# DeltaNet heads two at a time in lockstep, and windowed attention pipelined over its blocks

## The chip, the cores and the metric

The kernel runs on one core of one Trainium2 chip. Its time is the device time of one execution in microseconds; the median of several executions is given. The engines of the core work beside each other, each through its own queue in order: PE is TensorE (matrix products, results in PSUM), DVE is VectorE, ACT is ScalarE, POOL is GpSimd, and SP issues most of the DMA transfers.

## What is computed

One inference step of two layers over a prompt of 2048 tokens with 16 learned tokens ahead of it, and 8 sample tokens with states of their own. Layer AB projects its input once and feeds two branches: A, attention with a window of 128 positions, 8 query heads and 2 key heads; B, a gated DeltaNet of 4 heads. Layer C is a gated linear attention of 4 heads. The part that the change reorders, cut from the reference:

```python
def _gated_delta_chunked(q, k, v, beta, g, s0, lead):
    ...
    a_mat = jnp.where(strict, jnp.einsum('bnhik,bnhjk->bnhij', kbeta, kc) * decay, 0.0) + jnp.eye(CHUNK, dtype=F32)
    ...
    sol = lax.linalg.triangular_solve(a_mat, rhs, left_side=True, lower=True, unit_diagonal=True)
    ...
    def step(S, xs):
        u_c, w_c, qk_c, qd_c, kd_c, gl_c = xs
        v_new = u_c - jnp.einsum('bhck,bhkv->bhcv', w_c, S)
        o = jnp.einsum('bhck,bhkv->bhcv', qd_c, S) + jnp.einsum('bhij,bhjv->bhiv', qk_c, v_new)
        S = S * gl_c[..., None, None] + jnp.einsum('bhck,bhcv->bhkv', kd_c, v_new)
        return S, o

    S, o = lax.scan(step, s0.astype(F32), xs)

def _sink_attend(q, k, v, mask, sink):
    s = jnp.einsum('...qhgd,...khd->...hgqk', q.astype(F32), k.astype(F32)) * (A_HEAD_DIM ** -0.5)
    ...
    p = p / (jnp.sum(p, axis=-1, keepdims=True) + jnp.exp(sk - m))
    o = jnp.einsum('...hgqk,...khd->...qhgd', p, v.astype(F32))
```

## The kernel before

The tokens go through in four groups of 512; group 0 carries 24 more columns, the sample and the learned tokens. For each group the kernel does layer AB, its output projection (`ab_out`), layer C and its output projection.

Most of TensorE's work are the projections. `proj` (L492) takes each product in three matmuls, of a high and a low part of the weights and of the input, into PSUM tiles named `pp` (four of them). This is called bulk here. The rest goes into PSUM tiles named `pc`, in short bursts: for DeltaNet (`dn_head`, L1420) and for attention (`swa_pair`, L983). These are generators that run as side streams of the bulk: `bulk` (L399) adds the planned time of each piece of a projection to a clock, and whenever the clock has passed the due time of a stream it lets this stream emit its next step, which then says how long it is planned to take (the numbers of `DEF_LAT`, L32). Streams of one kind stand in a lane, one after another: a lane `dn` for the heads of DeltaNet, a lane `swa` for the pairs of attention heads. `join` (L418) emits steps until given streams have ended, with no bulk ahead of them. `ORDER` (L30) is the order in a group: the convolution and gates of a head (`c1`, `c2`, `c3`; `c0` comes ahead) in turn with the attention pairs (`s0` to `s3`). What is emitted so is then ordered on each engine by a scheduler, within its dependences. So the order on an engine is found from the planned clock, the due times and the pools.

Tiles of 512 columns (`T`, 52 of them, 47 to be taken by streams), and the larger `BQ` tiles (4) are counted by `take` and `give`; a stream that finds none waits in `take_in`, which steps on the clock by 0.5. Smaller pools are `t512` (4), `sm` (20) and `inv` (6).

A head of DeltaNet goes through these steps for the group's four chunks of 128 at once: transposes and norms of keys, the products of keys with keys and queries (`BQ`), an inversion of the triangular matrix (L1496 on), transposes of values and queries; then the scan, chunk by chunk, and a normalisation (L1608 to L1616) with the gate. The inversion starts with blocks of 32: in four stages, s = 2, 4, 8, 16, TensorE does 16 matmuls of 32x32 for the four chunks (`pc<-inv,t`), DVE multiplies with a mask (`Pm`), TensorE does 16 more (`pc<-inv,inv`), and DVE subtracts (`Yn`) and transposes (`X`). In the profile a matmul in fp32 shows as two records, so a burst of 16 is 32. In the scan a chunk needs the state S (`pc<-S,CQ`), a DVE operation (Z), a matmul (`pc<-t,t`), a copy on ACT, two more matmuls (`pc<-t,t`, `pc<-t,BQ`), and the new S on DVE.

A pair of attention goes over four blocks of 128 queries. `scores` is four matmuls (`pc<-kh,t`), then a maximum on DVE, the exponential on ACT and a division on DVE; `values` transposes the probabilities on TensorE (L1015) and copies them on ACT (L1017); `out` is the products with the values (`pc<-t,va`).

## Time and profile before

| | |
|---|---|
| median of 3 runs | 2223.04 us (2221.27 to 2227.0) |
| the profiled execution | 2224.94 us |
| its span, first to last instruction | 2223.2 us |
| granted TensorE clock, mean | 0.986 |
| HBM traffic | 297.19 MB read, 101.70 MB written, 179 GB/s over the span |

Busy time is the time in which an engine had an instruction under way. Matmuls overlap, so TensorE can be busy and still not at its peak. A row of a group gives line, engine, operation, output and inputs by name without buffer numbers, shape, count, then busy time, mean ns of one, and the idle time of the engine ahead of them with what ended it. A row of the timeline gives start, duration, the same names, a count where several stand in a line, and in brackets the idle time ahead of it.

### The profile page before, as it was taken

How to read it: one execution, taken by the hardware profiler on the slowest of the kernel's cores; microseconds unless marked ns; L12 is line 12 of the kernel's file. 1: busy time of each engine (PE TensorE's matmuls, PEld its weight loads, DVE VectorE, ACT ScalarE, POOL GpSimd, SP SyncE). 2: the span in 40 equal slices, each digit the busy share in tenths (PEclk: the TensorE clock that was granted, in tenths of full speed). 3: DMA queues.
4: the chain of work that ended last, by engine and by line, in shares of the span. 5: the costliest groups of instructions: out<-in, count | busy, mean ns of one | idle time of the engine just before them, and what ended most of it. 6: DMA issues, size and time to landing. Idle time of an engine off the chain costs nothing.

```text
span 2223.2 us, 43787 instructions
## 1 busy us (share of the span) xinstructions
PE 2152.0 (97%) x17290; PEld 1809.8 (81%) x17290; DVE 1231.0 (55%) x3501; ACT 835.4 (38%) x2235; POOL 263.6 (12%) x314
## 2 busy tenths in 40 slices
PE   8889999999999999999999999999999999999997
PEld 8878888888879777788887777788887877778886
DVE  7768876655464566544344466545344466654323
ACT  5435444443352244333332244334333233334222
POOL 0011100021210011002220011002130000001111
PEclk9989999999999999999999999999999999999999
DMA  6643537767766723464555733365554743274444
GB/s 236 211 155 121 175 118 263 253 218 261 253 204 244 242 96 103 135 239 142 181 204 164 267 107 102 125 218 169 180 198 147 245 147 114 86 259 156 157 149 156
DMA packets 162622, 400.17 MB, mean 180 GB/s; under 512 B 22048, under 2 KB 54464, under 8 KB 162384
## 3 DMA queue, kind: packets, MB, share of 16 engines
q1 hardware_dynamic: 162416, 397.37, 52.6%
q8 instruction: 136, 2.23, 0.4%
q14 instruction: 70, 0.57, 0.1%
HBM read 297.19 MB, written 101.70 MB: 179 GB/s over the span
## 4 chain that ended last, share of the span: by engine, by line
PE 69%; DVE 5%; DMA 2%; ACT 2%; issue 2%; POOL 1%; SPq 0%; DVEq 0%; POOLq 0%; ACTq 0%
PE pp L110 53%; PE pc L110 14%; DVE t L116 2%; DVE t L113 1%; DVE inv L113 1%; PE pc L1015 1%; DMA t<-in_xT 1%; PE pc L1796 1%; DMA t<-x2d 1%; POOL sm L206 0%; DVE t L120 0%; DVE t L999 0%; PE pc L1575 0%; PE pc L1450 0%; DMA t<-rows 0%
## 5 line engine op out<-in xcount | busy, mean ns | idle before, releaser
L110 PE MATMUL pp<-t,wh 128*128 128x512 f32 (+1 forms) x4528 | 1265.8, 364 | 17.7 <-DVE t L113 7.7
L110 PEld LDWEIGHTS pp<-t,wh 128*128 128x128 f32 x4528 | 782.6, 191 | 128.4 <-issue 19.6
L110 PE MATMUL pp<-t,wl 128*128 128x512 f32 (+1 forms) x2264 | 808.8, 358 | 1.9 <-DVE wl L113 1.7
L110 PEld LDWEIGHTS pp<-t,wl 128*128 128x128 f32 x2264 | 429.8, 190 | 60.5 <-DVE wl L113 2.7
L113 POOL TENSOR_TENSOR t<-t,t 128x512 fp32r<-128x512 f32 (+3 forms) x128 | 163.8, 1298 | 517.3 <-ACT t L660 275.1
L110 PE MATMUL pp<-wh,t 128*128 128x256 f32 (+1 forms) x1088 | 209.0, 288 | 3.8 <-DVE QKt L113 3.8
L116 DVE SCALAR_TENSOR_TENSOR t<-t,PV,t 128x512 f32<-128x512 f32 (+4 forms) x232 | 176.0, 768 | 60.0 <-ACT t L1098 24.3
L110 PEld LDWEIGHTS pp<-wh,t 128*128 128x128 f32 x1088 | 172.4, 190 | 6.0 <-DVE QKt L113 4.0
L206 POOL TENSOR_TENSOR sm<-sm,mh 128x2 f32<-128x2 f32 (+3 forms) x84 | 68.4, 814 | 812.3 <-DVE sm L116 367.5
L116 DVE SCALAR_TENSOR_TENSOR t<-pp,t 128x512 f32<-128x512 f32 (+3 forms) x160 | 93.1, 586 | 120.0 <-PE pp L110 67.5
L110 PE MATMUL pp<-wl,t 128*128 128x256 f32 (+1 forms) x544 | 155.8, 286 | 0.0
L113 DVE TENSOR_TENSOR wl<-raw,wh 128x512 fp32r<-128x512 f32 (+3 forms) x138 | 92.2, 685 | 23.3 <-PE pp L110 10.9
L110 PEld LDWEIGHTS pp<-wl,t 128*128 128x128 f32 x544 | 103.4, 190 | 0.6
L365 ACT CAST wh<-raw 128x512 fp32r<-128x512 f32 (+2 forms) x122 | 68.0, 588 | 50.6 <-DMA raw<-in_w_c 17.0
L113 DVE TENSOR_TENSOR t<-t,t 128x512 f32<-128x512 f32 (+4 forms) x103 | 62.9, 614 | 41.3 <-ACT t L489 40.0
L113 DVE TENSOR_TENSOR QKt<-pp,t 128x512 f32<-128x512 f32 (+1 forms) x40 | 23.3, 586 | 111.0 <-PE pp L110 95.6
L110 PEld LDWEIGHTS pc<-t,t 128*128 128x128 f32 (+4 forms) x496 | 62.9, 162 | 22.2 <-DVE t L116 4.0
L489 ACT ACTIVATE t<-t 128x512 f32<-128x512 f32 (+1 forms) x70 | 44.1, 631 | 97.5 <-DVE t L116 69.0
L1004 ACT ACTIVATE t<-t,sm 128x257 f32<-128x257 f32 x128 | 64.2, 504 | 43.4 <-DVE sm L116 42.7
L110 PE MATMUL pc<-t,t 128*128 128x128 f32 (+5 forms) x496 | 78.1, 267 | 1.6 <-DVE t L116 0.8
L113 DVE TENSOR_TENSOR t<-pp,t 128x268 f32<-128x268 f32 (+1 forms) x90 | 44.4, 497 | 50.3 <-PE pp L110 36.0
L1017 ACT COPY t<-pc 128x512 f32<-128x512 f32 x64 | 37.5, 586 | 79.5 <-PE pc L1015 77.7
(334 smaller groups left out, 2806.5 us busy)
## 6 DMA issues: line engine op xcount, KB each, us to landing
wh<-wd SPq DMA_DIRECT2D x157, 512.0 KB, 3.6
wl<-wd SPq DMA_DIRECT2D x157, 512.0 KB, 4.5
wd<-wh SPq DMA_DIRECT2D x55, 512.0 KB, 4.0
wd<-wl SPq DMA_DIRECT2D x55, 512.0 KB, 5.6
t<-in_xT SPq DMA_DIRECT2D x72, 256.0 KB, 4.6
raw<-in_w_ab SPq DMA_DIRECT2D x25, 512.0 KB, 5.7
raw<-in_w_c SPq DMA_DIRECT2D x16, 512.0 KB, 4.9
out_yp<-t SPq DMA_DIRECT2D x32, 256.0 KB, 2.5
```

Of the source, the lines that this page charges most:

```text
L110: T.matmul(out, lhsT, rhs, start=start, stop=stop)
L113: return (eng or V).tensor_tensor(out, a, b, op=op)
L116: V.scalar_tensor_tensor(out, a, s, b, op0=op0, op1=op1)
L206: G.tensor_tensor(out, x, mh[0:x.shape[0]].to_broadcast(list(x.shape)), op=ALU.pow)
L365: last[0] = A.copy(hi[:, c], raw[:, c])
L489: A.activation(sq[:, :q.C], x, AF.Square)
L1004: A.activation(S_[:, kv], S_[:, kv], AF.Exp, bias=st[:, 2 + kv:3 + kv], accum_out=st[:, 4 + kv:5 + kv])
L1015: T.transpose(pt[:, kv, x], S_[:, kv, 128 * x:128 * x + 128], ident)
L1017: A.copy(PT, pt)
L1796: T.transpose(oT[:, c], On[:, c, 128 * j:128 * j + 128], ident)
```

## The change

A new function `together` takes the streams of several heads and advances all of them by one step at a time; its step is planned to take the longest of theirs times `PAIR_LAT`, 1.25. In `ab_conv` the main chunks of heads 0 and 1, and of 2 and 3, are collected and spawned as one stream when the second of them has its queries and keys. The streams of the 16 learned tokens (group 0 only) stay one per head. A wait inside such a stream now yields `None`, which steps on by 0.5 and lets the other head of a pair wait with it.

`swa_pair` emits, for every pair but the last of `ORDER` (u = 3), in one step the `out` of block b - 2, the `values` of block b - 1 and the `scores` of block b, six steps in all, where it took one of them per step. The last pair is as before.

`BQ` tiles go from 4 to 6, `t512` from 4 to 8, `sm` from 20 to 24, `inv` from 6 to 10, and a scratch buffer for DMA descriptors is set to 1024. No arithmetic changes.

```diff
+NBQ = 6
+PAIR_LAT = 1.25
...
+    def together(gens):
+
+        gens = list(gens)
+        while gens:
+            lat, pe = [], 0.0
+            for gen in list(gens):
+                r = next(gen, False)
+                while r and r[0] is None:
+                    yield r
+                    r = next(gen, False)
+                if r:
+                    lat.append(r[0])
+                    pe += r[1]
+                else:
+                    gens.remove(gen)
+            if lat:
+                yield max(lat) * PAIR_LAT if len(lat) > 1 else lat[0], pe
...
         while not cond():
-            yield 0.5, 0.0
+            yield None, 0.0
...
-                s = spawn(chunks(), "dn", LAT["dn_spawn"], tag=h)
-                q.dn.append(s)
+                q.pair.append(chunks())
+                if h % 2:
+                    q.dn.append(spawn(together(q.pair), "dn", LAT["dn_spawn"], tag=h))
+                    q.pair = []
...
+        if u == int(ORDER[-1][1]):
...
+        else:
+
+
+            PT = {}
+            for i in range(6):
+                if i >= 2:
+                    out(i - 2, PT.pop(i - 2))
+                if 1 <= i <= 4:
+                    PT[i - 1] = values(i - 1)
+                if i < 4:
+                    scores(i)
+                if i == 3:
+                    give("T", 2)
+                yield LAT["sw_p"], (1.35 if 2 <= i <= 3 else 0.9 if i in (1, 4) else 0.45)
...
-        tc4 = lambda: wk.tile([128, 4, 32], F32, tag="inv", bufs=6, name=nm("inv"))
+        tc4 = lambda: wk.tile([128, 4, 32], F32, tag="inv", bufs=10, name=nm("inv"))
...
-    nc = _bacc.Bacc("TRN2", target_bir_lowering=False, num_devices=1)
+    nc = _bacc.Bacc("TRN2", target_bir_lowering=False, num_devices=1, dynamic_dma_scratch_size=1024)
```

What this makes of the order on TensorE is shown at three places. The numbers behind a name tell instances of it apart; rows into `pp` are bulk, one matmul each. Lines of the changed kernel lie two further down here (L110 is L112).

First TensorE in the inversion of a head, group 1, before: `pc<-inv,inv` and `pc<-inv,t` are the two kinds of burst of a stage.

```order
L110 MATMUL pc_9785<-inv_9802,inv_9777 32x32 x16
L110 MATMUL pp_9968<-t_8092,wl_9832 128x512
L110 MATMUL pp_9968<-t_8103,wh_9831 128x512
L110 MATMUL pp_9968<-t_8104,wh_9831 128x512
L110 MATMUL pc_9842<-inv_9804,t_9697 32x32 x16
L110 MATMUL pp_9968<-t_8103,wl_9832 128x512
L110 MATMUL pp_9968<-t_8123,wh_9831 128x512
L110 MATMUL pp_9968<-t_8124,wh_9831 128x512
L110 MATMUL pc_9842<-inv_9859,inv_9827 32x32 x16
```

And the changed kernel in the inversion of a pair of heads, the same group (9375 and 9382 are the matrices of the two heads):

```order
L112 MATMUL pc_9524<-inv_9541,inv_9500 32x32 x16
L112 MATMUL pc_9544<-inv_9561,inv_9519 32x32 x16
L112 MATMUL pc_9613<-inv_9543,t_9375 32x32 x16
L112 MATMUL pp_9881<-t_8131,wh_9655 128x512
L112 MATMUL pc_9633<-inv_9563,t_9382 32x32 x16
L112 MATMUL pc_9613<-inv_9630,inv_9587 32x32 x16
L112 MATMUL pc_9633<-inv_9650,inv_9606 32x32 x16
L112 MATMUL pc_9707<-inv_9632,t_9375 32x32 x16
```

A burst of one head had three bulk matmuls behind it; now bursts of two heads stand in turn, with one bulk matmul in a stage here, and up to three in others.

Second, TensorE in the last scan of group 0, before, with the state S_48 of head 3 (one chunk's first bursts):

```order
L110 MATMUL pc_4421<-S_48_170,CQ_3295 128x128 x2
L110 MATMUL pp_4531<-t_103,wl_4405 128x268
L110 MATMUL pp_4531<-t_107,wh_4404 128x268
L110 MATMUL pp_4531<-t_108,wh_4404 128x268
L110 MATMUL pp_4531<-t_107,wl_4405 128x268
L110 MATMUL pp_4531<-t_111,wh_4404 128x268
L110 MATMUL pp_4531<-t_112,wh_4404 128x268
L110 MATMUL pp_4531<-t_111,wl_4405 128x268
L110 MATMUL pc_4421<-t_4270,t_3693 128x128
L110 MATMUL pp_4531<-t_115,wh_4404 128x268
L110 MATMUL pp_4531<-t_116,wh_4404 128x268
L110 MATMUL pp_4531<-t_115,wl_4405 128x268
```

And the changed kernel there, with the states S_47 and S_48 of heads 2 and 3 (a chunk, and the start of the next):

```order
L112 MATMUL pc_5091<-S_47_168,CQ_2187 128x128 x2
L112 MATMUL pc_5095<-S_48_170,CQ_3000 128x128 x2
L112 MATMUL pc_5091<-t_4987,t_4288 128x128
L112 MATMUL pc_5095<-t_4994,t_4296 128x128
L112 MATMUL pc_5109<-t_966_5100,t_3299 128x128
L112 MATMUL pc_5109<-t_966_5100,BQ_4301 128x128
L112 MATMUL pc_5114<-t_968_5105,t_4281 128x128
L112 MATMUL pc_5114<-t_968_5105,BQ_4307 128x128
L112 MATMUL pc_5119<-S_47_168,CQ_2187 128x128 x2
L112 MATMUL pc_5123<-S_48_170,CQ_3000 128x128 x2
```

The bulk matmuls between the bursts are gone here; the long run of them for the output projection follows after the normalisation of both heads. In groups 1 to 3 the scans of a pair keep bulk between them.

Third, DVE in group 0 ahead of an eviction of bulk (`t<-pp,t`), before; `sm_1804` is a small tile of the sample tokens, `wl` the low part of a weight, split on DVE from what ACT has cast to `wh`:

```order
L116 SCALAR_TENSOR_TENSOR t_367_1816<-pc_1791,sm_1804,t_366_1814 8x128
L116 SCALAR_TENSOR_TENSOR sm_1855<-sm_1855 32x1
L113 TENSOR_TENSOR t_1446<-t_1446,sm_1855 32x128
L116 SCALAR_TENSOR_TENSOR t_365_1805<-t_367_1816,sm_1804,t_365_1805 8x128
L113 TENSOR_TENSOR wl_1910<-raw_1905,wh_1909 128x512
L116 SCALAR_TENSOR_TENSOR sm_1804<-sm_1804 8x1
L113 TENSOR_TENSOR wl_2140<-raw_2135,wh_2139 128x512
L120 TENSOR_SCALAR t_365_1805<-t_365_1805,sm_1804 8x128
L113 TENSOR_TENSOR t_1831<-pp_1676,t_232 128x268
```

And the changed kernel ahead of the like eviction (`sm_1805`; `inv` and `CC` with `t_1233` and `t_1241` belong to the inversions of heads 0 and 1):

```order
L118 SCALAR_TENSOR_TENSOR sm_1805<-sm_1805,egs_196 8x1
L115 TENSOR_TENSOR inv_1785<-inv_1687,pc_1766 128x128
L118 SCALAR_TENSOR_TENSOR t_362_1817<-pc_1792,sm_1805,t_361_1815 8x128
L1563 STREAM_TRANSPOSE inv_1879<-inv_1785 128x128
L118 SCALAR_TENSOR_TENSOR sm_1829<-sm_1829 32x1
L115 TENSOR_TENSOR t_1233<-inv_1765,CC_92 128x128 x2
L118 SCALAR_TENSOR_TENSOR t_360_1806<-t_362_1817,sm_1805,t_360_1806 8x128
L115 TENSOR_TENSOR t_1204<-t_1204,sm_1829 32x128
L115 TENSOR_TENSOR t_1233<-inv_1765,CC_92 128x128 x2
L122 TENSOR_SCALAR inv_1909<-pc_1900 32x128 x2
L115 TENSOR_TENSOR t_1241<-inv_1785,CC_92 128x128 x2
L115 TENSOR_TENSOR t_1841<-pp_1567,t_232 128x268
```

The two weight splits ahead of the eviction stand further up now, ahead of the sample's operations, and steps of two inversions have come between.

## The prediction

> **What bounds the kernel now.** I read the page first, then the table of waits, then single stretches of the timeline. Lines of the page (engine busy, share of the span; then the chain that ended last):

> ```profile
> PE 2152.0 (97%) x17290; PEld 1809.8 (81%) x17290; DVE 1231.0 (55%) x3501; ACT 835.4 (38%) x2235; POOL 263.6 (12%) x314
> PE 69%; DVE 5%; DMA 2%; ACT 2%; issue 2%; POOL 1%; SPq 0%; DVEq 0%; POOLq 0%; ACTq 0%
> PE pp L110 53%; PE pc L110 14%; DVE t L116 2%; DVE t L113 1%; DVE inv L113 1%; PE pc L1015 1%; DMA t<-in_xT 1%; PE pc L1796 1%; DMA t<-x2d 1%; POOL sm L206 0%; DVE t L120 0%; DVE t L999 0%; PE pc L1575 0%; PE pc L1450 0%; DMA t<-rows 0%
> ```

> TensorE is the bound, and over half of the chain is the projections, the matmuls into `pp`, called bulk below. So the change can win only what TensorE spends beside the matmuls: places where it changes from bulk to a side burst (into `pc`) and back, and waits. Windows (length, then busy time of PE, PEld, DVE, ACT, POOL, with counts; granted clock; DMA) say where waits are:

> ```profile
> 0.00:400.00 400.00, 369.00 (x3831) 333.32 (x3832) 305.36 (x1067) 186.29 (x560) 35.33 (x51) 0.95 0.55 186
> 650.00:970.00 320.00, 314.39 (x2916) 253.70 (x2915) 186.73 (x535) 117.09 (x340) 24.72 (x38) 1.00 0.52 177
> 970.00:1170.00 200.00, 199.57 (x1144) 173.72 (x1143) 83.09 (x180) 70.90 (x151) 39.66 (x39) 1.00 0.51 177
> ```

> The first 400 us, roughly layer AB of the first group of tokens, idle 31 us; layer AB of the second (650 to 970) idles 5.6; a layer C (970 to 1170), which the change hardly touches, 0.4. The largest waits of TensorE on the parts in question (total, times, longest) and one on the timeline:

> ```profile
> PE pc L110 <- DVE inv L113: 13.4, 17, 1.8
> 143.56 0.79 PE L110 MATMUL pp<-t,wh 128*128 128x268 f32 x2 [5.92 <-DVE t L113]
> ```

> **Inversion bursts.** The order of TensorE shows 693 uninterrupted runs of bulk before and 501 after, with the same matmuls. Places where bulk is left for a 32-wide burst fall from 163 to 86: 77 fewer. The timeline of one head's inversion, second group:

> ```profile
> 668.39 0.45 PE L110 MATMUL pc<-inv,inv 32*32 32x32 f32 x32
> ...
> 668.92 0.29 DVE L113 TENSOR_TENSOR inv<-inv,pc 128x128 f32<-128x128 f32 x1 [0.50 <-PE pc L110]
> ...
> 669.25 0.28 PE L110 MATMUL pp<-t,wh 128*128 128x268 f32 x1
> 669.46 0.45 PE L110 MATMUL pc<-inv,t 32*32 32x32 f32 x32
> 669.85 0.39 PE L110 MATMUL pp<-t,wh 128*128 128x268 f32 x1
> 669.99 0.29 DVE L113 TENSOR_TENSOR inv<-pc,CC 128x128 f32<-128x128 f32 x1 [0.44 <-PE pc L110]
> 670.08 0.29 PE L110 MATMUL pp<-t,wl 128*128 128x268 f32 x1
> 670.20 0.41 PE L110 MATMUL pp<-t,wh 128*128 128x268 f32 x2
> ```

> A bulk matmul of this width starts 0.12 us after the last (670.08 to 670.20). The one ahead of the burst holds 0.21 (669.25 to 669.46), 0.09 more. The row of all such bursts gives 0.197 us for one matmul:

> ```profile
> L110 PE MATMUL pc<-inv,t 32*32 32x32 f32 x2328 | 39.8, 197 | 12.6 <-DVE inv L113 12.1 <-issue 0.2
> ```

> So the last of the 32 starts 0.45 - 0.20 = 0.25 after the first, and bulk only at 0.39: 0.14 more. The first bulk matmul then holds 0.23 (669.85 to 670.08) in place of 0.12: 0.11 more. One visit costs 0.34 us beside its work, and 77 fewer save **26 us**.

> The pair's chain works against it. From a burst's start to the DVE operation on its result is 0.53 us (668.39 to 668.92, and 669.46 to 669.99; DVE stood idle for PE both times), that takes 0.29, and DVE's end to the next PE start is 0.05 (S in the next fence: 691.87 + 0.34, then 692.26). A stage has two such halves: 2 x 0.87 = 1.74 us. After the change TensorE has, in a stage of a pair, four bursts of 0.25 and mostly one bulk matmul, with its switches about 0.46: 1.46 us. The missing 0.28 us is a new wait, over 4 stages x 2 pairs x 4 groups = 32 stages **+9 us**; 0 where two more bulk matmuls stand between, 32 x 0.74 = 24 where none does. The 13.4 us of waits listed are 17, and there are 16 heads in four groups: I read them as one at the start of each inversion. A pair has one start in place of two: half would be -7, and I take **-5** (0 to -9), since a pair's start has more to wait for.

> **Wide bursts.** The other 115 of the 192 runs saved are 128-wide bursts of the scan and attention (scan of a head, all engines):

> ```profile
> 690.81 0.49 PE L110 MATMUL pc<-t,t 128*128 128x128 f32 x2
> ...
> 691.14 0.39 PE L110 MATMUL pc<-t,BQ 128*128 128x128 f32 x2
> 691.28 0.49 PE L110 MATMUL pp<-t,wh 128*128 128x268 f32 x2
> ...
> 691.61 0.29 PE L110 MATMUL pp<-t,wl 128*128 128x268 f32 x1
> 691.73 0.41 PE L110 MATMUL pp<-t,wh 128*128 128x268 f32 x2
> 691.87 0.34 DVE L116 SCALAR_TENSOR_TENSOR S<-S,el,pc 128x128 f32<-128x128 f32 x1
> 691.98 0.29 PE L110 MATMUL pp<-t,wl 128*128 128x268 f32 x1
> ...
> 692.26 0.71 PE L110 MATMUL pc<-S,CQ 128*128 128x128 f32 x4
> ...
> 693.01 0.35 DVE L116 SCALAR_TENSOR_TENSOR t<-pc,sm,t 128x128 f32<-128x128 f32 x1 [0.60 <-PE pc L110]
> ```

> Two bulk matmuls after the burst take 0.33 (691.28 to 691.61), later 0.25: 0.08 is lost per visit. But a burst that another burst follows takes 0.33 (690.81 to 691.14), one that bulk follows 0.14: the switch is paid all the same. I take **0**, from -0.08 x 115 = -9 to +0.11 x 115 = +13.

> **The end of group 0.** Here the order shows the scan of heads 2 and 3 with no bulk at all between its bursts, where before each head's bursts had 3 to 7 bulk matmuls between. TensorE must then wait out the chain. Rows of the rest of that chain:

> ```profile
> 693.91 0.39 PE L110 MATMUL pc<-t,t 128*128 128x128 f32 x2
> ...
> 694.33 0.27 ACT L1593 COPY t<-pc 128x128 f32<-128x128 f32 x1 [1.49 <-PE pc L110]
> ...
> 695.24 0.38 PE L110 MATMUL pc<-t,t 128*128 128x128 f32 x2
> ...
> 696.13 0.35 DVE L116 SCALAR_TENSOR_TENSOR S<-S,el,pc 128x128 f32<-128x128 f32 x1
> ```

> One chunk without bulk: 0.75 to the DVE operation (692.26 to 693.01), 0.35, 0.42 from the next burst to ACT (693.91 to 694.33), 0.27, 0.89 to S (695.24 to 696.13), 0.35, and three times 0.05: 3.2 us. TensorE's own bursts are about 0.47 (690.81 to 691.28), 0.47 for S,CQ by the same spacing, and 0.2: 1.1 a head, 2.2 a pair. So 1.0 us idle in each of 4 chunks, 4 us. Then the normalisation, with all of a head's steps in a line:

> ```profile
> 699.93 0.39 PE L110 MATMUL pc<-t,BQ 128*128 128x128 f32 x2
> ...
> 701.62 1.01 POOL L206 TENSOR_TENSOR sm<-sm,mh 128x4 f32<-128x4 f32 x1 [42.06 <-DVE sm L116]
> ...
> 702.67 0.69 DVE L113 TENSOR_TENSOR t<-t,sm 128x512 f32<-128x512 f32 x1 [1.12 <-POOL sm L206]
> ```

> From the last burst to the end of the DVE product: 703.36 - 699.93 = 3.4 us, and the second head's POOL operation is 1.0 later: 4.4 us with nothing for TensorE. Before, 60 us around this place idled 3.3 us, which go:

> ```profile
> 270.00:330.00 60.00, 56.67 (x691) 49.77 (x683) 47.55 (x202) 27.37 (x95) 4.43 (x5) 1.00 0.36 114
> ```

> Net 4 + 4.4 - 3.3 = **+5** (0 to +15, if the same pair's inversion, which stands among attention bursts, waits too). In groups 1 to 3 the scan keeps 1 to 9 bulk matmuls between bursts, and only the last attention pair is left at the end with about 4 between: I take 1.3 us a group, under half of those 3.3, **+4** for the three (0 to +12).

> **The stall at 143.56 and the clock.** Its windows:

> ```profile
> 137.00:143.00 6.00, 0.64 (x5) 0.40 (x4) 4.09 (x20) 4.98 (x18) 2.16 (x3) 0.70 0.24 86
> 143.50:147.00 3.50, 3.31 (x17) 3.03 (x21) 3.37 (x11) 1.65 (x4) 0.00 (x0) 0.50 0.87 216
> 150.00:160.00 10.00, 10.00 (x264) 8.42 (x263) 6.70 (x24) 0.83 (x2) 0.00 (x0) 0.85 0.73 255
> ```

> After 5.92 us idle the clock is 0.50 from 143.5 to 147 and 0.85 over 150 to 160, which is 3 us of half speed there; with 147 to 150 between, 9.5 us at half speed, up to 4.7 us lost. The wait itself was DVE's queue: an eviction of `pp` behind operations of the sample tokens and two weight splits that wait for ACT. In the new order the splits stand further ahead of that eviction, and a pair's inversion beside it. I take half of 5.92 + 4.7: **-5** (0 to -11). The idle 4.4 us at the end of group 0 could do the same to the clock: waits up to 1.8 us left it at 1.00 and 5.9 halved it, so I take **+2** (0 to +4.7).

> [...]

> The other edits move nothing by themselves: more buffers of `BQ`, `t512`, `sm` and `inv` let two heads live at once, the smaller DMA scratch pays for them, and the polling steps issue no instruction. What they could cost is room: pairs take their tiles in a block, which is the drain below.

> **Sum.** -26 + 9 - 5 + 0 + 5 + 4 - 5 + 2 = -16 us. The profiled run took 2224.94 us (its span 2223.2); it becomes 2209. The median of the runs, 2223.04, lies 1.9 below it: **2207 us**.

> **Rivals.** (1) *The pairs' chain is the bound*: no bulk is left between the bursts of a stage, 24 in place of 9: -1 us, 2222. For it: before, DVE already waited 0.44 and 0.50 for PE in each half, so nothing is slack. Against: the order has a bulk matmul in most stages. (2) *The drain*, slower: both heads of a pair end together, so at each output projection, not only in group 0, the pair's scan and normalisation have no bulk beside them: 8.4 us idle and 4.7 of half clock in each of four groups is 52, where the sum has 5 + 4 + 2; -16 + 41 = +25, 2248. It decides where the last bulk matmul is issued before the pair's first chunk; the order shows that for group 0, and bulk in the others, which speaks against it. (3) *The waits go as well*: the stall at 143.56 and its clock wholly (-11), the inversion waits (-9), no new one in the stages (0): -16 - 6 - 4 - 9 = -35, 2188. For it: DVE is 55% busy and the two heads cover each other. That the change doesn't pair the heads is excluded by the order.

> **Numbers.** Forecast (2199 to 2216) 0.45, rival 1 (2216 to 2230) 0.22, drain 0.16, rival 3 (2180 to 2199) 0.17. A measurement tells about 0.3%, 6.7 us, from no change: faster 0.62, same 0.22, slower 0.16. The range leaves out the lower half of rival 3 and the upper part of the drain: 2190 to 2238.

> **What would show it.** Bulk entries to 32-wide bursts fall and waits of `pc` on DVE `inv` stay near 13 us: forecast; they grow by 10 or more: rival 1. Layer AB of the second group should be 5 to 7 us shorter; if it isn't, the price of a visit is wrong. Idle of TensorE before the first output projection (270 to 330) over 10 us with a clock below 1.00: the drain. The stall near 143 gone: rival 3. Wrong altogether would be a slower layer C, or waits on a DMA.

## The result, and the profile after

The changed kernel takes 2302.05 us in the median of 4 runs (2297.99 to 2310.96), beside 2222.26 us before (2221.27 to 2227.0): a ratio of 1.0363, 95% interval 1.0337 to 1.039. It is 80 us slower, where 16 us faster was forecast. The profiled execution took 2310.96 us. Its page, engine busy and the chain that ended last:

```profile
PE 2195.0 (95%) x17290; PEld 1859.5 (81%) x17290; DVE 1225.4 (53%) x3501; ACT 833.5 (36%) x2235; POOL 265.2 (11%) x314
PE 55%; DVE 5%; issue 3%; DMA 3%; ACT 2%; POOL 1%; SPq 0%; DVEq 0%; POOLq 0%; ACTq 0%
```

TensorE does the same 17290 matmuls and is busy 43 us longer; its idle time grew from 71 to 114 us. And "issue", time in which an engine waits for nothing that the profile shows, stands in the chain with 3%, where it had 2%. The table of waits of TensorE (total, times, longest) names it first:

```profile
PE pc L112 <- issue: 21.2, 17, 2.7
PE pc L112 <- DVE inv L115: 11.4, 13, 2.9
PE pp L112 <- DMA wl<-wd: 8.8, 3, 3.3
PE pc L1039 <- DVE t L122: 8.5, 14, 0.9
```

The waits on DVE's `inv`, which the prediction took as the danger, did not grow (13.4 us before). Waits on a DMA (`wl<-wd`), which it named as a sign of being wrong altogether, are new. The windows that answer to the three shown of before (the same layers, which lie later now; the columns are the window, its length, the busy time and count of PE, PEld, DVE, ACT and POOL, the granted clock, the share of DMA and its GB/s):

```profile
0.00:400.00 400.00, 361.13 (x3631) 323.17 (x3632) 290.34 (x1036) 178.46 (x544) 33.98 (x50) 0.91 0.50 168
673.00:1003.00 330.00, 314.26 (x2878) 256.38 (x2878) 180.73 (x529) 113.91 (x336) 24.91 (x37) 0.94 0.48 164
1013.00:1187.00 174.00, 173.50 (x996) 150.99 (x995) 68.82 (x149) 60.03 (x126) 38.09 (x34) 1.00 0.51 182
```

The granted clock in layer AB of the second group is 0.94 now, and was 1.00; layer C is as it was. Cut at the starts of the same bulk matmuls of the trace, near the borders of the layers, the time lies so (us; the experiments are told below). For the noise of one trace: e3 below, which has neither pairs nor the pipelined attention, differs from the kernel before by 6 us in C 0 and by under 3 in every other column.

```
                          AB 0   C 0    AB 1   C 1    AB 2   C 2    AB 3   C 3
before                    380.8  244.6  327.6  184.4  349.1  181.8  328.7  204.7
after                     405.9  242.9  346.3  184.6  369.0  181.5  350.5  205.1
e1_pair_only              402.0  238.4  340.5  185.0  369.3  180.6  340.2  205.2
e2_swa_only               380.7  237.4  328.2  185.1  346.1  184.8  325.3  204.8
e4_half_issue             400.7  240.3  327.4  185.7  351.2  180.9  328.2  204.8
e5_spread                 390.8  241.9  336.2  184.5  360.4  183.9  332.7  204.7
e6_keep_busy              392.3  239.0  341.6  184.7  362.0  181.2  343.4  204.9
e8_spread_g0_single       380.7  241.2  337.3  184.2  363.0  181.5  334.6  204.7
e9_half_g0_single         388.1  237.3  326.9  184.8  348.5  183.5  328.0  205.0
e10_before_half           383.6  242.9  327.8  184.5  346.5  180.9  327.7  205.2
e11_scan_pair             374.5  236.2  324.0  184.6  345.1  182.3  322.3  204.6
```

All four layers AB lost 19 to 25 us. The place in each is the inversion of a pair. TensorE on the timeline of the first pair of group 1 (start, length, operation, output and inputs, size, count, and in brackets the idle time ahead and what ended it):

```profile
778.09 0.45 PE L112 MATMUL pc<-inv,t 32*32 32x32 f32 x32
778.36 0.81 PE L112 MATMUL pc<-inv,inv 32*32 32x32 f32 x33
781.74 0.60 PE L112 MATMUL pc<-inv,inv 32*32 32x32 f32 x28 [2.56 <-issue]
782.13 0.24 PE L112 MATMUL pc<-inv,t 32*32 32x32 f32 x1
782.14 0.25 PE L112 MATMUL pc<-inv,inv 32*32 32x32 f32 x3
782.18 0.63 PE L112 MATMUL pc<-inv,t 32*32 32x32 f32 x31
782.74 0.80 PE L112 MATMUL pp<-t,wh 128*128 128x512 f32 x1
783.47 0.65 PE L112 MATMUL pc<-inv,t 32*32 32x32 f32 x32
783.92 0.63 PE L112 MATMUL pc<-inv,inv 32*32 32x32 f32 x32
785.46 0.65 PE L112 MATMUL pc<-inv,inv 32*32 32x32 f32 x32 [0.92 <-DVE inv L1563]
785.92 0.62 PE L112 MATMUL pc<-inv,t 32*32 32x32 f32 x32
786.47 0.80 PE L112 MATMUL pp<-t,wl 128*128 128x512 f32 x1
787.19 0.65 PE L112 MATMUL pc<-inv,t 32*32 32x32 f32 x32
```

From the one bulk matmul of a stage (782.74) to that of the next (786.47) are 3.7 us, twice the 1.74 of the prediction. TensorE breaks off at 779.2, with 33 of the 64 records of the two heads' bursts done, and goes on 2.56 us later. The second head's burst had begun, and the rest of it needs nothing that its first matmul didn't. The bulk matmul then takes 0.80 us in place of 0.50, and from 780 on the clock is at about half:

```profile
776.00:780.00 4.00, 3.05 (x153) 2.10 (x139) 2.73 (x10) 0.00 (x0) 0.00 (x0) 1.00 0.92 352
780.00:792.00 12.00, 8.69 (x324) 6.56 (x324) 5.46 (x24) 0.00 (x0) 0.00 (x0) 0.54 0.04 12
```

What breaks a burst is told by a queue that the prediction did not read. The page's part on DMA queues has an instruction queue q8; the trace has 136 records of it, 16384 bytes each, and 136 x 256 is just above 2 x 17290, the matmuls and weight loads of TensorE: blocks of 256 instructions, by division 64 bytes each. The rows above agree: from 781.74 up to 785.46 are 128 matmuls (28 + 1 + 3 + 31 + 1 + 32 + 32), with their weight loads 256 instructions, and there TensorE stops again. The profile puts these 0.92 us down to a transpose on DVE; but the next stop, at 788.92, is "issue" again and another 256 instructions on. In the whole run, stops for "issue" that follow each other in one pair's inversion stand a block apart, without exception. In the stretch above the blocks start at 779.3, 782.8, 786.6 and 790.1 us. Data transfers do not hold them up there: the window from 780 has the DMA engines busy for a share of 0.04. Over the whole run no two are closer than 3.33 us; before, the closest were 3.35. A stage of a pair is four bursts of 32 matmuls and 32 weight loads, 256 instructions: one block, 3.5 to 3.8 us. Before, a head's stage had 128 and those of 6 or 7 bulk matmuls, some 140 in 2.5 us: a block lasted by this about 4.5 us. That was enough: before, TensorE's waits for "issue" are 0.2 us, in one place.

### The profile page after: what moved, and what is told of

Its sections match the earlier page's. It is cut to its first block, busy times and chain, and to the rows that moved or that the text cites. A ratio compares the mean times of both kernels' runs of the same rounds, so it can differ in the third digit from the quotient of the medians.

```text
span 2309.1 us, 43811 instructions
## 1 busy us (share of the span) xinstructions
PE 2195.0 (95%) x17290; PEld 1859.5 (81%) x17290; DVE 1225.4 (53%) x3501; ACT 833.5 (36%) x2235; POOL 265.2 (11%) x314
## 4 chain that ended last, share of the span: by engine, by line
PE 55%; DVE 5%; issue 3%; DMA 3%; ACT 2%; POOL 1%; SPq 0%; DVEq 0%; POOLq 0%; ACTq 0%
PE pp L112 42%; PE pc L112 11%; DMA t<-x1d 2%; DVE t L118 2%; DVE t L115 1%; POOL sm L208 1%; PE pc L1039 1%; DMA wl<-wd 1%; DVE inv L115 1%; DVE t L122 1%; ACT junk L1492 1%; PE pc L1834 0%; ACT t L1028 0%; DVE t L1023 0%; DMA t<-x2d 0%
## 5 line engine op out<-in xcount | busy, mean ns | idle before, releaser
L112 PE MATMUL pp<-t,wh 128*128 128x512 f32 (+1 forms) x4528 | 1276.1, 367 | 16.2 <-ACT t L152 7.7
L112 PEld LDWEIGHTS pp<-t,wh 128*128 128x128 f32 x4528 | 803.1, 194 | 139.0 <-issue 14.1
L112 PE MATMUL pp<-t,wl 128*128 128x512 f32 (+1 forms) x2264 | 815.3, 360 | 11.6 <-DMA wl<-wd 8.8
L112 PEld LDWEIGHTS pp<-t,wl 128*128 128x128 f32 x2264 | 438.0, 194 | 73.3 <-DMA wl<-wd 10.1
L112 PE MATMUL pp<-wh,t 128*128 128x256 f32 (+1 forms) x1088 | 208.3, 287 | 3.8 <-DVE QKt L115 3.8
L112 PEld LDWEIGHTS pp<-wh,t 128*128 128x128 f32 x1088 | 171.7, 190 | 5.9 <-DVE QKt L115 4.0
L112 PE MATMUL pp<-wl,t 128*128 128x256 f32 (+1 forms) x544 | 155.4, 286 | 0.0
L208 POOL TENSOR_TENSOR sm<-sm,mh 128x4 f32<-128x4 f32 (+3 forms) x84 | 68.8, 819 | 680.8 <-DVE sm L124 279.3
L112 PEld LDWEIGHTS pp<-wl,t 128*128 128x128 f32 x544 | 103.3, 190 | 0.7
L112 PE MATMUL pc<-t,t 128*128 128x128 f32 (+5 forms) x496 | 76.5, 276 | 1.1 <-DMA t<-in_sdn 0.4
L112 PEld LDWEIGHTS pc<-t,t 128*128 128x128 f32 (+4 forms) x496 | 63.0, 170 | 14.0 <-issue 3.6
L112 PEld LDWEIGHTS pc<-inv,t 32*32 32x32 f32 x2328 | 38.5, 128 | 44.3 <-issue 29.5
```

Source lines behind the costliest of these rows:

```text
L112: T.matmul(out, lhsT, rhs, start=start, stop=stop)
L208: G.tensor_tensor(out, x, mh[0:x.shape[0]].to_broadcast(list(x.shape)), op=ALU.pow)
```

## The experiments

Three theories. *Supply*: a pair's inversion needs instructions faster than they come. *Clock*: the granted clock falls in small bursts without bulk, and the half clock is the loss. *Drain*: the pairs end late, and groups end with TensorE empty. Each kernel ran against the kernel before on the same chip; the ratio's 95% interval is in brackets.

**Parts of the change.** One edit each puts `swa_pair` back (e1), puts the heads back (e2), or both, so that only pools, caps, scratch and polling are left (e3):

```diff
-        if u == int(ORDER[-1][1]):
+        if True:
```
```diff
-                q.pair.append(chunks())
-                if h % 2:
-                    q.dn.append(spawn(together(q.pair), "dn", LAT["dn_spawn"], tag=h))
-                    q.pair = []
+                s = spawn(chunks(), "dn", LAT["dn_spawn"], tag=h)
+                q.dn.append(s)
```

> The changed kernel without the pipelined attention; heads still paired. Supply theory: in a pair's inversion TensorE runs out of instructions (the records of its instruction queue, 16 KB or 256 instructions each, come there every 3.4 to 3.8 us and never closer than 3.3, and a stage of a pair needs 256 and takes 3.7 us where its data would allow 1.74), so the loss stays with the pairs: 2285 to 2305 us, gaps without a data releaser about 20 us. Clock theory (the pair's small bursts look idle to the clock gate, and the half clock is the loss): the same time, mean clock 0.95 to 0.96. Drain theory (the loss is at the ends of the groups, where the attention comes late): under 2265 us.

Measured 2286.52 us, ratio 1.0291 (1.0271 to 1.0312), mean clock 0.960, gaps of "issue" 25.8 us in 19. The loss is with the pairs, which is against drain.

> The changed kernel with its heads one by one as before; the attention pipelined, the larger pools kept. Supply and clock theories: 2212 to 2226 us, mean clock 0.985, since the runs of bulk fall only from 693 to 661 and the inversions keep bulk between their bursts. Drain theory: 2240 us or more.

Measured 2213.89 us, 0.9971 (0.9955 to 0.9987), clock 0.987. The pipelined attention alone is a small gain, near the low end of the range.

> Only the larger pools, the caps, the smaller DMA scratch and the polling; no pair and no pipelined attention. All three theories: 2217 to 2228 us. If the DMA scratch or the pools were the cause it would be over 2240.

Measured 2218.53 us, 1.0000 (0.9987 to 1.0013). Pools and scratch cost nothing.

**Half the instructions (e4).** The changed kernel, in both loops of the four stages:

```diff
-            for c in range(nch):
+            w2 = 2 if L == 128 else 1
+            for c in range(0, nch, w2):
...
-                    MM(pi[r, 0, c], Ap[r, c, 32 * a:32 * a + 32], Y[r, c])
+                    MM(pi[r, 0, c:c + w2], Ap[r, c, 32 * a:32 * a + 32], Y[r, c:c + w2])
```

> The changed kernel with half the matmul instructions in the inversion's four stages: each multiplies 64 columns, of two chunks, with the weights of the first of them, in place of 32 of each chunk with its own, so the odd chunks are not inverted. As many columns are streamed as before. Supply theory: a stage of a pair needs 128 instructions, the gaps without a releaser fall from 21 us to under 6, 2240 to 2265 us. Clock theory: what the array does is the same, so the half clock stays (mean 0.95 to 0.96) and the time with it, 2290 to 2310 us.

Measured 2237.15 us, 1.0069 (1.0046 to 1.0091), clock 0.977: 65 us of the 80 are gone, though as many columns stream; it is 3 us below the range of the supply theory. "issue" no longer stands among the nine largest waits of TensorE. The timeline of a stage, from one double burst to the next:

```profile
768.01 0.65 PE L112 MATMUL pc<-inv,inv 32*32 32x64 f32 x32
768.59 0.50 PE L112 MATMUL pp<-t,wl 128*128 128x512 f32 x1
769.02 0.43 PE L112 MATMUL pc<-inv,t 32*32 32x64 f32 x16
769.38 0.49 PE L112 MATMUL pp<-t,wh 128*128 128x512 f32 x1
769.80 0.43 PE L112 MATMUL pc<-inv,t 32*32 32x64 f32 x16
770.15 0.51 PE L112 MATMUL pp<-t,wh 128*128 128x512 f32 x1
770.59 0.65 PE L112 MATMUL pc<-inv,inv 32*32 32x64 f32 x32
```

2.6 us, with three bulk matmuls in it, at full clock (0.50 a bulk matmul). In the table above the layers AB of groups 1 to 3 are back at the kernel before. Group 0 keeps 20 of its 25 us: its loss is not the supply in the main. Its granted clock over 320 to 380 us is still 0.72.

**The supply by itself (e7).** The kernel before, and behind its last product:

```diff
+            pb_ = sm()
+            V.tensor_copy(pb_, Y[3][:, 1, 0:32])
+            po = cb((128, 16, 32))
+            for i in range(512):
+                r = slice(32 * (i % 4), 32 * (i % 4) + 32)
+                MM(po[r, i // 4 % 16], ident[r, r], pb_[r])
```

> The kernel before with 512 independent fp32 matmuls of 32x32 added after its last product, 1024 matmul and 1024 weight-load instructions in the trace's count, with nothing beside them; their results are not read. Supply theory: 2048 instructions are 8 blocks of 256, at one per 3.3 to 3.8 us they take 24 to 30 us, in runs with gaps without a releaser, and the kernel is 20 to 28 us longer. Clock and drain theories: at the 8 ns spacing of a burst they take 8 to 9 us, up to 17 at half clock, without gaps.

Measured 2248.28 us, 1.0125 (1.0107 to 1.0144): 29 us more, 1 over the supply theory's range. TensorE at the end of its timeline, with nothing to wait for:

```profile
2222.55 1.93 PE L110 MATMUL pc<-sm,CC 32*32 32x32 f32 x128 [2.29 <-issue]
2226.30 1.93 PE L110 MATMUL pc<-sm,CC 32*32 32x32 f32 x128 [1.82 <-issue]
2230.32 1.92 PE L110 MATMUL pc<-sm,CC 32*32 32x32 f32 x128 [2.09 <-issue]
```

128 matmuls, which with their weight loads are 256 instructions, then a gap of 1.82 to 2.29 us, and so on to the end: a block each 3.75 us in the mean. The 512 matmuls of the code are 1024 in the trace, and q8 has 144 blocks in place of 136: 8 x 256 is 2 x 1024. This settles the supply. (The granted clock is 0.50 here, over 2218 to 2248 us; the gaps are the supply's all the same: in the changed kernel TensorE broke off at 779.2 us with the clock at 1.00.)

Ahead of these rows TensorE stood idle for 2.88 us, then went through 171 of the probe's matmuls, 342 instructions, and stopped for the first time.

**Clock without supply (e6).** The changed kernel; `keep` stands behind each burst of the four stages:

```diff
+            def keep():
+                for _ in range(2 if L == 128 else 0):
+                    MM(pw[:, 256:512].rearrange("p (c t) -> p c t", c=2), identb, bcm(negb, 2))
```

> The changed kernel with 256 matmuls added that nobody reads: after each 32-wide burst of the four stages two of 128x256 in bf16 into the free half of its PSUM tile, some 0.1 us each, 28 us of TensorE in all, and 4 instructions to a burst's 64. They keep the array busy without easing the supply. Clock theory: the mean clock returns to 0.98 or more and the time falls in spite of the work, to 2285 us or less. Supply theory: gaps without a releaser stay at 15 us or more, and the time is 2295 to 2325 us.

Measured 2279.36 us, 1.0270 (1.0243 to 1.0297), clock 0.987. The time is in the clock theory's range, not in that of the supply theory; but gaps of "issue" are still 14.8 us in 19, just under what the supply theory said. By the ratios some 21 us are gone, in spite of an estimated 28 us of added work (256 matmuls of 256 columns; in the trace of before a bulk matmul of 268 starts 0.12 us after the last). By the trace's clock records the kernel before runs 65 us at half clock in 9 periods, the changed one 219.6 in 22, this one 59 in 11. So the half clock was part of the loss, at least those 21 us. It was not all of it: e6 has no more half clock than the kernel before and is 60 us slower, 32 more than the added work. And the supply's limit is not a matter of the clock: from 880 to 890 us the clock of e6 is 1.00, the blocks come 3.5 us apart all the same, and a burst stops for 0.91 us.

Half the clock can also last without idle time. In group 0 of the changed kernel it begins at 330 us, behind a wait of 2.89 us, and lasts 17 us; a window of this, with a pair's inversion among attention and some bulk, has TensorE busy throughout:

```profile
336.00:344.00 8.00, 8.00 (x262) 6.70 (x254) 5.68 (x29) 2.02 (x6) 0.00 (x0) 0.50 0.35 132
```

So the profile's busy time alone does not tell the clock: 8.00 of 8.00 us here, about half of them in 32-wide bursts, stayed at half of it. That such bursts do less than wide matmuls to keep it up would fit e6, where wide matmuls behind each burst brought the half clock from 219.6 us to 59; the gaps became shorter there too (14.8 us in place of 21.2), so this isn't shown by itself.

**More bulk between (e5), and group 0 (e8, e9).** e5 plans the inversion's steps wider; e8 is e5, and e9 is e4, with heads one by one in group 0:

```diff
+                wide = 2.2 if max(lat) in (LAT["dn_ia"], LAT["dn_ib"]) else PAIR_LAT
-                yield max(lat) * PAIR_LAT if len(lat) > 1 else lat[0], pe
+                yield max(lat) * wide if len(lat) > 1 else lat[0], pe
```
```diff
-                if h % 2:
+                if h % 2 or g == 0:
```

> The changed kernel with one number changed: the eight steps of a pair's four stages of inversion are planned to take 2.2 times a head's step in place of 1.25, so that more bulk comes between the bursts of both heads; the same matmuls in another order. Supply theory: a stage then lasts longer than 256 instructions take to arrive, gaps without a releaser under 8 us, 2230 to 2260 us, clock 0.97 or more. Drain theory: pairs end still later in their groups, 2300 us or more.

Measured 2256.66 us, 1.0165 (1.0148 to 1.0183), clock 0.976, gaps 12.0 us in 9, more than said: bursts of both heads still stand beside each other. 45 us are gone, which is against drain.

> As the kernel with the spread steps (2.2 times in the inversion), and group 0's heads one by one; pairs in groups 1 to 3 only. Drain theory for group 0, where the trace of the changed kernel lost some 25 us: 10 to 25 us below the kernel with the spread steps alone, 2210 to 2240 us. If group 0 lost its time to the supply of instructions alone: within 6 us of it.

Measured 2248.75 us, 1.0129 (1.0103 to 1.0154): 8 us less than e5, which is between the two theories' figures, and above the 2210 to 2240 us. Layer AB of group 0 is at 380.7, as before.

> The changed kernel with half the matmul instructions in the inversion (the odd chunks are not inverted) and group 0's heads one by one. With half the instructions and pairs everywhere, groups 1 to 3 came back to the kernel before within 2 us each and group 0 kept 20 us. If that rest is the pair's end in group 0 (the scan with no bulk beside it): 2212 to 2224 us. If it is something else in group 0, such as the attention's order or the pools: 2230 us or more.

Measured 2227.18 us, 1.0026 (1.0003 to 1.0049), between the two ranges: most of group 0's rest is gone, but its layer AB is still 7 us over the kernel before in the profiled run. What these 7 are was not followed.

**Pairing without the supply (e10), and in the scan only (e11, e12).** e10 is the kernel before with e4's edit. In e11, `together` takes each head alone up to a mark that stands ahead of the scan; e12 adds group 0 as in e8:

```diff
+        for gen in gens:
+            for r in gen:
+                if r[0] == "scan":
+                    break
+                yield r
         while gens:
...
+        if L == 128:
+            yield "scan", 0.0
         yield from until(lambda: L == 32 or first)
```

> The kernel before, heads one by one, with the same half of the matmul instructions in the inversion (the odd chunks are not inverted). It prices pairing without the supply: against the kernel with pairs and half the instructions, whose layers AB of groups 1 to 3 took 327, 351 and 328 us. If a visit to a 32-wide burst costs the 0.34 us predicted, unpaired heads are 4 us or more a group longer, in sum over 1019 us. If pairing saves nothing, 1000 to 1010 us, and the whole kernel 2205 to 2220.

Measured 2219.34 us, 0.9985 (0.9967 to 1.0003); layers AB of groups 1 to 3 sum to 1002 us, beside 1007 in e4 and 1003 in e9. Pairing the inversions saves nothing even when instructions are plenty, all the less as e4 and e9 have the pipelined attention as well, which alone gave 6 us. The run is also the control of e4: without pairs, half the instructions change nothing, so the 65 us there are not for less work.

> The changed kernel with the two heads of a pair going through keys, inversion and values one after the other, and in lockstep only from the scan on; nothing is left out. Supply theory: inversions have bulk between their bursts again, gaps without a releaser under 5 us, layers AB of groups 1 to 3 within 5 us of the kernel before each, group 0 still 5 to 20 us longer, 2215 to 2245 us. If pairing costs by its late ends and its room rather than by the inversion: over 2260.

Measured 2203.15 us, 0.9910 (0.9875 to 0.9945), clock 0.993: faster than both kernels, and better than any theory said, in group 0 too. TensorE is busy 16 us less than before and idle 11 us less. No "issue" among the seven largest waits; its page:

```profile
PE 2135.7 (97%) x17290; PEld 1808.9 (82%) x17290; DVE 1215.4 (55%) x3501; ACT 836.3 (38%) x2235; POOL 263.4 (12%) x314
```

> As the kernel with pairs in the scan only, and group 0's heads one by one. Supply theory, with the end of group 0 taken away: 2205 to 2222 us, at best below the kernel with the pipelined attention alone (2214). If the scan's lockstep itself costs: over 2230.

Measured 2205.97 us, 0.9924 (0.9897 to 0.9950): not to be told from e11. The scan's lockstep costs nothing in group 0.

## Why the prediction was wrong

**The failing step** is "The pair's chain works against it": a stage of 1.74 us, from TensorE's time and the data's path, +9 us. The stage shown took 3.7 us, since it holds 256 instructions and the blocks of these came 3.3 to 4.8 us apart in the pairs' inversions. Layers AB of groups 1 to 3 became 60 us longer, 2.5 for each of their 24 stages, and with half the instructions 59 of these are gone. The bound was in the trace of before: 136 blocks in q8, none closer than 3.35 us, and some 140 instructions in 2.5 us in a head's stage, near that rate already. The rivals had a bound of the data's chain and of empty ends, none of the instructions themselves.

**The clock** was weighed at one place, the end of group 0 (+2). It fell in every pair's inversion: 219.6 us at half clock in place of 65. If TensorE's speed had bound all of these 154 us they would be 77 us of loss, which is an upper estimate; TensorE's idle time for "issue" is 21 us. The two overlap, since TensorE is idle at half clock as well (3.3 of the 12 us from 780 on, at 0.54), and how the 80 us divide is open. e6 only bounds it: 21 us or more are the clock's, and some 32 come without it. The reading that "waits up to 1.8 us left it at 1.00" passed over a place in the trace of before: the first inversion of group 0 (59 to 68 us) goes with no bulk between its bursts and with waits of 1.66 us at most, and from 61 to 71 us the clock is 0.50. The closest two blocks of that trace, 3.35 us apart, start there too, the first at 63.3 us.

**The 26 us for visits to 32-wide bursts** did not come. Visits fell as the order said, but between e10 and e9, both with half the instructions, groups 1 to 3 differ by 1 us, where three quarters of -26 + 9 is -13. Over the whole run TensorE is busy 10 us less in e9 (2139.2 beside 2149.6), so a part of the saving was there, but it is idle 13 us more. These are not waits for DVE's `inv`, which are 10.3 us in e9 and 13.1 in e10. The new ones are 8.7 us of attention bursts for DVE (`t`, ahead of L1039) and 8.7 for weights (`wl<-wd`).

**The waits at an inversion's start, -5**, were misread: 8 of the 17, 4.9 of the 13.4 us, lie in that one inversion, between 59 and 68 us, so they are not one for each head. The sum fell only to 11.4.

**Wide bursts at 0** (-9 to +13): here was the gain. Pipelined attention gave 6 us in the sum of groups 1 to 3 (e2: 999.6, before 1005.4), scans in lockstep 8 more (e11: 991.4), in all 14, more than the low end. That it came by the price of the switches was not tested.

**The end of group 0, +5**, came out as part of +25. Its cause was put at the scan; e11 has the paired scan there and no loss, so it was the pair's way up to the scan. Its clock is low (0.78 over 300 to 360 us), and so it is in e4 (0.72 over 320 to 380 us) with half the instructions; that the clock is the main cause there is likely, not shown. **The stall at 143.56** did go, but gaps of "issue" at 123 and 129 us and their half clock took its place; layer AB of group 0 shows no gain of it. In e11 the term came true: the wait is 1.1 us, the clock from 100 to 160 us is 1.00, and layer AB of group 0 is 6 us shorter; e12, with group 0's heads one by one, keeps the 5.9 us. **Groups 1 to 3's ends, +4**: e4 and e9 leave no room for more than 2 us.

**Rivals.** Drain gave the nearest time, 2248, by luck, and isn't what happened: in e11 both heads of a pair still scan and end together, with the same pools, and it is faster. Rival 1 had the right place and the wrong bound.

Open: why the pipelined attention costs 16 us beside pairs (e1 to the changed kernel) and gains 6 without them, and the three waits on `wl<-wd` of some 3 us each ahead of layers C, which stand in e1, e4 and e9 too, and are shorter in e2 and e11 (some 4 to 6 us in all). Open is also why no block comes sooner than 3.3 us after the last.

## What to carry to other kernels

Count instructions as well as time where small matmuls are packed closer: here TensorE got 256 in 3.3 to 4.8 us in the pairs' inversions, and where it needed more it stopped in the middle of a burst, with "issue" as its releaser (17 times, 21.2 us). Large matmuls between small bursts were no waste here: before, with 6 or 7 of them, a stage needed only some 140 instructions in 2.5 us, "issue" was 0.2 us, and the clock in layer AB of the second group was 1.00 in place of 0.94. Before steps of two streams are put side by side, ask which of them wait for data, as a scan does, and which are long in instructions, as the inversion is; here only the first gained.
